# A hybrid decoder layer on one core: the gate product in column groups, work moved to the front, stage offsets redrawn

## The chip, the core and the metric

The kernel runs on one core of one Trainium2 chip. The time is device microseconds of one execution; lower is better. Three executions of the kernel before took 2729.17, 2730.89 and 2732.62 us. A further execution, 2731.02 us long, was taken with the hardware profiler, and all views of the trace come from it.

## What is computed

One decoder layer (DEPTH is 1, so only layer 0 of the reference runs) on x of 2048 tokens by 1024, with a memory of 256 rows. Token mixer (gated DeltaNet, 8 heads of 128) and memory attention (4 heads) share one input projection and one output projection; then come layer norm, an MLP with squared ReLU (1024 to 4096 to 1024), and a second layer norm.

```python
proj = x @ w_in
a = proj[..., 4 * GDN_WIDTH:4 * GDN_WIDTH + GDN_HEADS]
b = proj[..., 4 * GDN_WIDTH + GDN_HEADS:4 * GDN_WIDTH + 2 * GDN_HEADS]
q = l2_normalize(heads(qkv[..., :GDN_WIDTH]))      # qkv after a causal conv and silu
beta = jax.nn.sigmoid(b.astype(jnp.float32))
g = -jnp.exp(a_log) * jax.nn.softplus(a.astype(jnp.float32) + dt_bias)
o = chunk_gated_delta_rule(q, k, v, g, beta)
o = (rms_norm(o, gate_norm_w) * jax.nn.silu(heads(z))).reshape(B, T, GDN_WIDTH)
m = memory_attention(mq, mem_k, mem_v)
return jnp.concatenate([o, m], axis=-1) @ w_out
```

The columns a and b of the projection, 16 in all, are what this text calls the gates: a decay and a write strength for each head and token.

## The kernel before, in words

**Stages.** Tokens are taken in four blocks of 512 (TB); two blocks make a pair. For each block the mixer runs over the 8 heads: `dense` projects q, k and v of a head and convolves them, `gdn_a` and `gdn_b` run the recurrence in chunks of 128, `gate` projects z, and four memory heads stand among them. After two mixers come the output projection (`out_seven`) and the two MLP matrices (`ff1`, `ff2`), each as a seven-product scheme, for the pair. The next pair follows. In the trace the first pair's mixers lie at about 0 to 570 us, its output projection up to about 760, its MLP up to about 1374, and the second pair repeats this.

**Precision.** A float32 operand is split into a high part, rounded to fp32r by ScalarE (`split`, line 555), and a low part, the rest, subtracted by VectorE. A product is three fp32r matmuls, high by high, high by low and low by high (`mm3`, line 573). Products with smaller operands, and all transposes, are plain float32. `T` is the split x of a block, transposed, in eight tiles k of 128 rows each (T_tiles, line 649); a weight pair (high and low) is a tile `whl`, its raw form `wraw` (three buffers). PSUM has banks of 512 columns: three for "acc", one "m", two "pb", and "ga0" and "ga1".

**The gates before.** `gates` (line 726) loads the 16 columns of the weight (w_ab), splits them into a tile abw of 16 high and 16 low columns, and multiplies: for each of the 8 k, abw by high T and by low T, 16 matmuls with 32 weight columns and 512 moving columns, all into partitions 0 to 31 of one acc bank (aab, lines 731 to 734). ScalarE copies the bank to ab, four transposes of 32 by 128 bring it to pab, and two VectorE operations add the parts for high and low weights into gab (lines 742 and 743). A chain of small operations then makes the decays and strengths, and matmuls with a triangle and with ones sum them (pg). All later stages of the block read them.

**The start.** `first_tokens` (line 1587) loads x of block 0 tile by tile, and between the tiles, in three pieces (W0K), q's weights of head 0; it splits each as it comes. `columns` loads four norm vectors and transposes them (pln); then come the gates, and then `mixer`, whose first projection (aq) uses the weights that `first_tokens` brought. k's weights of head 0 come through `load_in` (line 586) when `dense` asks for them: for block 0 this loads the raw weights, splits them and stores the split form (wsc), and other blocks load that.

**Later blocks.** `next_block` (line 1608) has five steps. Steps 0 to 3 load two x tiles each into one wraw buffer and split them; step 4 loads q's weights of head 0 and makes the gates. For blocks 1 and 3 the five steps stand behind the previous mixer; for block 2 they stand inside the last product of the first pair's `ff2`.

**The order of the work.** Nothing is issued as written. A recorder keeps all operations, and `issue` (line 313) plays them through a planner with a cost for each (`cost`, line 272): each engine takes, of the operations whose inputs are ready by the plan, the one with the lowest number. The number is the place in the program plus an offset. `PLACE` (line 190) holds these offsets for named stages, keyed by block, step and letter; `spot` (line 529) switches them. The resulting order is fixed in the program, and each engine runs its list in that order. Almost every operation therefore has line 424 in the trace, and groups are told apart by tile names: aq, ak, av, az and amq are projections, pc, po, pkq, pq and pp belong to the recurrence, ao is the output projection, fA to fC and f2A to f2C the MLP.

Of the kernel before, what the change touches and what calls it, by code (L numbers as in the profile page):

```python
# [184 lines left out]
class Op:  # L185
# [2 lines left out]


PLACE = {  # L190
# [12 lines left out]
}  # L203


class Recorder:
# [64 lines left out]
    @staticmethod  # L271
    def cost(o, name, wr, rd, args, kw):
        e = o.eng
        shapes = [r.shape for r in wr] + [r.shape for r in rd]
        n = max([_prod(s[1:]) for s in shapes] or [1])
        if e == "PE":
            rhs = kw.get("rhs", args[2])
            mo, n = _prod(args[1].shape[1:]), _prod(rhs.shape[1:])
            f32 = name == "transpose" or isinstance(rhs, Ref) and rhs.buf.dtype == F32
            o.load, o.cols, o.lhs = 4 + 0.84 * mo, mo, args[1].buf if isinstance(args[1], Ref) else None  # L280
            o.last = 2.4 + 0.8334 * n if f32 else 13.4 + 0.4167 * n
            if name == "transpose":
                return o.last
            if f32:
                return o.last + max(o.last, o.load)
            return o.last
        psum = any(r.buf.psum for r in rd + wr)
        if e == "SP":
            n = _prod(wr[0].shape if wr else rd[0].shape)
            o.extra = 1700 + n * 4 / 300.0  # L290
            o.late = 2000 if rd and any(s[0] == "partition_broadcast" for s in rd[0].steps) else 300
            return 450
        scal = [v for v in args[2:] if not isinstance(v, (int, float))] if name.startswith("tensor_scalar") else []
        scal += [v for k, v in kw.items() if k in ("scalar", "scalar1", "scale", "bias") and not isinstance(v, (int, float))]
        if e == "ACT":
            n = _prod((wr[0]).shape[1:])
            return 52 + 0.833 * n + (0 if psum else 42) + 93 * len(scal) + ((305 if scal else 198) if "accum_out" in kw else 0)
        if e == "DVE":
            slow = 30 if name in ("transpose", "stream_shuffle") else 0
            fast = not psum and not any(r.perm() for r in rd + wr) and name in ("tensor_copy", "tensor_scalar_mul", "tensor_scalar_add", "tensor_scalar_max",  # L300
                                         "memset")
            return 68 + slow + (0.52 if fast else 1.042) * n + 62 * len(scal) + (7 * n if name == "reciprocal" else 0)
        if name == "memset":
            return 40 + 0.83 * n
        if kw.get("op") == ALU.pow:
            return 460 + 165 * n
        if name == "tensor_copy":
            return 120 + 0.83 * n
        if name == "affine_select":
            return 125 + 0.9 * n  # L310
        return 150 + 2.1 * n if name == "tensor_tensor" else 296 + 3.34 * n
# [129 lines left out]
def hybrid_layer(  # L441
# [46 lines left out]
    def small(name, shape, bufs=3, dt=F32):  # L488
        return rec.buf(sm, shape, dt, name, bufs, name)

    def bank(name, tag):
        return rec.buf(ps, (P, TB), F32, tag, PBUFS[tag], name)
# [39 lines left out]
    state = [rec.buf(cst, (P, P), F32, "state%d" % h, 1, "state") for h in range(H)]  # L532
    for h in range(H):
        nc.gpsimd.memset(state[h], 0.0)
    lnc = rec.buf(cst, (P, 4 * KT), F32, "lnc", 1, "lnc")
    nea = rec.buf(cst, (P, H), F32, "nea", 1, "nea")
    halo = rec.buf(cst, (P, 24, 3), F32, "halo", 1, "halo")
# [185 lines left out]
                                  in_=st[i].bitcast(F32).rearrange("p (h e) -> p h e", h=MH))  # L723


    def gates(b, T):
        raw = small("abraw", [P, KT, 16], 1)
        nc.sync.dma_start(out=raw, in_=w_ab.rearrange("p (k f) -> p k f", k=KT))
        w = small("abw", [P, KT, 32], 1, F32R)
        split(raw, w[:, :, :16], w[:, :, 16:])  # L730
        a = bank("aab", "acc")
        for k in range(KT):
            nc.tensor.matmul(a[:32], w[:, k], T_of(T, 0, k), start=k == 0, stop=False)
            nc.tensor.matmul(a[:32], w[:, k], T_of(T, 1, k), start=False, stop=k == KT - 1)
        ab = slot("ab", "th")
        nc.scalar.copy(out=ab[:32], in_=a[:32])
        pab = bank("pab", "m")
        for c in range(NC):
            nc.tensor.transpose(pab[:, c * 32:(c + 1) * 32], ab[:32, c * P:(c + 1) * P], ident[:32, :32])
        pc = pab[:, :P].rearrange("p (c f) -> p f c", c=NC)  # L740
        pv = small("gab", [P, 16, NC], 1)
        nc.vector.tensor_copy(pv, pc[:, 16:])
        nc.vector.tensor_tensor(out=pv, in0=pc[:, :16], in1=pv, op=ALU.add)
        sh = [P, H, NC]
        if b == 0:
            alog = small("alog", [P, H], 1)
# [76 lines left out]
    def dense(b, h, T, G, w0=None):  # L823
        res = {}
        for nm, o in (("q", QO), ("k", KO), ("v", VO)):
            w = w0 if w0 and nm == "q" else load_in(b, o // P + h)
            a = bank("a" + nm, "acc")
            project(a, w, T)
            c = slot("c" + nm, "d")
# [315 lines left out]
    MEMORY = 1  # L1145
    MEM_AT = {5: 0, 6: 1, 7: 2, 8: 3}

    W0K = {0: 2, 2: 4, 4: 8}

# [435 lines left out]
        nc.vector.tensor_copy(lnc, pt[:, :4 * KT])  # L1585

    def first_tokens():
        T = T_tiles()
        rt = rec.buf(wp, (P, KT, P), F32, "wraw", NR, "wraw")
        wt, hi, lo = pair()  # L1590
        hi, lo = hi.rearrange("p (k f) -> p k f", k=KT), lo.rearrange("p (k f) -> p k f", k=KT)
        for k in range(KT):
            if k % 2 == 0:
                xj = tok_tile("xj").rearrange("p (k f) -> p k f", k=2)
            if k in W0K:
                w = slice(k, W0K[k])
                kw = range(k, W0K[k])
                nc.sync.dma_start(out=rt[:, w].part(*kw), in_=w_in[0].rearrange("p (k f) -> p k f", k=KT)[:, w])
                split(rt[:, w].part(*kw), hi[:, w].part(*kw), lo[:, w].part(*(100 + i for i in kw)))
            xk = xj[:, k % 2].part(k % 2)  # L1600
            nc.sync.dma_start(out=xk, in_=xtd[:, k, 0:TB])
            split(xk, T_of(T, 0, k), T_of(T, 1, k))
        nc.sync.dma_start(out=wsc[0], in_=wt.bitcast(F32))
        return T, ([hi[:, k].part(k) for k in range(KT)], [lo[:, k].part(100 + k) for k in range(KT)])

    ahead = {}

    def next_block(b, step):

        if b >= NB:  # L1610
            return
        if step < 4:
            if step == 0:
                ahead["T"] = T_tiles()
            k = 2 * step
            xj = rec.buf(wp, (P, 1024), F32, "wraw", NR, "xj").rearrange("p (k f) -> p k f", k=2)
            nc.sync.dma_start(out=xj, in_=xtd[:, k:k + 2, b * TB:(b + 1) * TB])
            split(xj, *(t[step] for t in ahead["T"]))
        else:
            ahead["w0"] = load_in(b, 0)  # L1620
            ahead["G"] = gates(b, ahead["T"])


    def mixer(b, T, w0, G):
# [184 lines left out]
    for s in range(NB // 2):  # L1809
# [5 lines left out]
        for i in range(2):  # L1815
            b = 2 * s + i
            if b == 0:
                T, w0 = first_tokens()
                columns()
                G = gates(b, T)  # L1820
            else:
                T, w0, G = ahead["T"], ahead["w0"], ahead["G"]
            mixer(b, T, w0, G)
            if i == 0:
                for k in range(5):
                    next_block(b + 1, k)
# [59 lines left out]
```

## Time and profile before

| what | value |
|---|---|
| three runs, median (lowest to highest) | 2730.89 us (2729.17 to 2732.62) |
| the profiled execution | 2731.02 us |
| its span in the trace | 2729.3 us |
| instructions in the span | 42448 |
| mean granted TensorE clock | 0.999 |
| HBM traffic over the span | 224 GB/s |

The span runs from the first instruction to the last; the remaining 1.7 us lie around it. PE is TensorE's matmuls, PEld its weight loads, which overlap them; DVE is VectorE, ACT is ScalarE, POOL is GpSimd, SP is the queue that issues nearly all DMAs. A busy time is the union of an engine's instructions. A matmul's own duration is its latency; in a row of them the distance between two starts is what each costs.

### The profile page before, as it was taken

The page shows a single profiled execution, that of the slowest core. Times are in us where ns is not written, and L with a number is a line of the kernel's source. Part 1 is how long each engine was busy: PE and PEld are TensorE (multiplying, and loading weights), DVE is VectorE, ACT ScalarE, POOL GpSimd, SP SyncE. Part 2 cuts the span into 40 slices and gives each one's busy share as a digit, 9 for nine tenths or more (in the row PEclk, how much of TensorE's full clock was granted, in tenths as well). Part 3 has the DMA queues.
Part 4 walks back from the last instruction along what each step waited for, and adds up shares of the span by engine and source line. Part 5 has one row for each costly group of instructions (what it writes and reads, how often), then busy time and mean ns, then how long its engine had stood idle before and what let it go on. Part 6 is the DMA issues. An engine that isn't in the chain of part 4 may idle for free.

```text
span 2729.3 us, 42448 instructions
## 1 busy us (share of the span) xinstructions
PE 2707.3 (99%) x13605; PEld 2265.5 (83%) x13605; DVE 2106.6 (77%) x5644; ACT 1634.3 (60%) x4106; POOL 414.5 (15%) x1030
## 2 busy tenths in 40 slices
PE   9999999999999999999999999999999999999998
PEld 7888888888888888888888888888887888888887
DVE  7999889998877777655778887888878666567575
ACT  7778767776475555333446676777756655553341
POOL 3233223321000000000023221332201000000000
PEclk9999999999999999999999999999999999999999
DMA  8666548867787879765754445345678643476673
GB/s 321 232 222 229 206 177 293 309 244 267 264 307 282 296 271 311 261 219 194 263 212 147 140 163 185 140 147 173 217 264 287 228 165 137 162 277 224 212 237 114
DMA packets 208543, 613.99 MB, mean 225 GB/s; under 512 B 23072, under 2 KB 32192, under 8 KB 188352
## 3 DMA queue, kind: packets, MB, share of 16 engines
q1 hardware_dynamic: 207888, 611.23, 63.7%
q8 instruction: 107, 1.75, 0.3%
q14 instruction: 116, 0.95, 0.1%
q10 hardware_dynamic: 432, 0.05, 0.0%
HBM read 436.54 MB, written 174.65 MB: 224 GB/s over the span
## 4 chain that ended last, share of the span: by engine, by line
PE 92%; DVE 3%; ACT 3%; POOL 1%; issue 1%; DMA 1%; DVEq 0%; SPq 0%; POOLq 0%; ACTq 0%
PE f2A L424 13%; PE fA L424 13%; PE ao L424 8%; PE f2C L424 6%; PE fC L424 6%; PE av L424 6%; PE aq L424 6%; PE ak L424 6%; PE az L424 5%; PE f2B L424 3%; PE fB L424 3%; PE amq L424 3%; PE pc L424 3%; PE po L424 2%; PE pkq L424 2%; PE pq L424 1%
## 5 line engine op out<-in xcount | busy, mean ns | idle before, releaser
L424 DVE TENSOR_TENSOR whl<-wraw,whl 128x512 fp32r<-128x512 f32 (+2 forms) x294 | 257.0, 884 | 112.5 <-ACT whl L424 109.6
L424 ACT CAST whl<-wraw 128x512 fp32r<-128x512 f32 (+2 forms) x294 | 226.6, 780 | 158.6 <-PE fC L424 54.6
L424 PE MATMUL fA<-B,whl 128*128 128x512 f32 x1152 | 278.9, 389 | 0.0
L424 ACT CAST X<-X 128x1024 fp32r<-128x1024 f32 x118 | 123.9, 1052 | 231.2 <-DMA X<-xsc 203.2
L424 PE MATMUL f2A<-whl,X 128*128 128x512 f32 x1152 | 262.1, 389 | 0.0
L424 PEld LDWEIGHTS fA<-B,whl 128*128 128x128 f32 x1152 | 216.1, 188 | 45.3 <-DVE B L424 0.3
L424 PEld LDWEIGHTS f2A<-whl,X 128*128 128x128 f32 x1152 | 216.3, 188 | 44.8
L424 DVE TENSOR_TENSOR X<-X,X 128x1024 fp32r<-128x1024 f32 x118 | 144.0, 1221 | 128.8 <-ACT X L424 128.8
L424 PE MATMUL aq<-T,whl 128*128 128x512 f32 x768 | 216.5, 409 | 6.5 <-ACT T L424 5.5
L424 PE MATMUL av<-T,whl 128*128 128x512 f32 x768 | 221.9, 405 | 1.0 <-DVE Bc L424 1.0
L424 PE MATMUL az<-T,whl 128*128 128x512 f32 x768 | 222.8, 404 | 0.0
L424 PE MATMUL ak<-T,whl 128*128 128x512 f32 x768 | 210.8, 405 | 0.0
L424 PE MATMUL fC<-B,whl 128*128 128x512 f32 x768 | 186.8, 389 | 0.4 <-DVE B L424 0.4
L424 PE MATMUL f2C<-whl,X 128*128 128x512 f32 x768 | 174.7, 389 | 0.0
L424 PEld LDWEIGHTS fC<-B,whl 128*128 128x128 f32 x768 | 144.0, 188 | 31.0 <-DVE B L424 0.8
L424 PEld LDWEIGHTS f2C<-whl,X 128*128 128x128 f32 x768 | 144.2, 188 | 29.9
L424 PEld LDWEIGHTS aq<-T,whl 128*128 128x128 f32 x768 | 136.8, 191 | 28.7 <-ACT T L424 5.5
L424 PEld LDWEIGHTS av<-T,whl 128*128 128x128 f32 x768 | 137.8, 189 | 24.2 <-ACT mst L424 1.4
L424 PEld LDWEIGHTS ak<-T,whl 128*128 128x128 f32 x768 | 137.3, 189 | 23.5
L424 PEld LDWEIGHTS az<-T,whl 128*128 128x128 f32 x768 | 137.9, 189 | 22.3
L424 POOL TENSOR_SCALAR ve<-mv 128x1 f32<-128x1 f32 x34 | 16.8, 493 | 918.3 <-DVE mv L424 917.8
L424 PE MATMUL ao<-whl,X 128*128 128x512 f32 x528 | 139.9, 404 | 0.3 <-DVE whl L424 0.3
(294 smaller groups left out, 6294.3 us busy)
## 6 DMA issues: line engine op xcount, KB each, us to landing
whl<-wsc SPq DMA_DIRECT2D x108, 1024.0 KB, 4.9
wraw<-in_w_ff_dram SPq DMA_DIRECT2D x106, 512.0 KB, 4.4
X<-xsc SPq DMA_DIRECT2D x96, 512.0 KB, 3.9
wsc<-whl SPq DMA_DIRECT2D x36, 1024.0 KB, 6.5
whl<-tsc SPq DMA_DIRECT2D x64, 512.0 KB, 4.6
xsc<-hB SPq DMA_DIRECT2D x96, 256.0 KB, 3.8
xo<-cat SPq DMA_DIRECT2D x80, 256.0 KB, 4.3
wraw<-in_w_in_dram SPq DMA_DIRECT2D x35, 512.0 KB, 6.0
```

The costliest lines, as they stand in the source:

```text
L424: o.fn(*[res(a) for a in o.args], **{k: res(v) for k, v in o.kw.items()})
```

## The change

There are four edits.

1. **The gate product.** `gate_rows` multiplies the raw float32 x tiles, not their split form, by the 16 weight columns, padded with zeros to 32, as plain float32 matmuls. Of the 8 tiles k, tile k goes to partitions 32 (k mod 4) to 32 (k mod 4) + 31 of the bank, so four column groups of TensorE are used in turn, and each accumulates two k. `gates` then copies all 128 rows, transposes four times 128 by 128, and four VectorE reductions add the four groups. The weights are loaded once into a constant tile, which GpSimd clears first; their split is gone. In blocks 1 and 3 the products come in two batches of four, after steps 1 and 3; in block 2, in one batch of eight after step 3, and x comes there in eight single tiles in "s0" slots; in block 0, in one batch after the eighth tile.
2. **Ten constant matmuls** (ones by ones, 128 columns, float32) stand first in `first_tokens`, into the bank "m".
3. **k's weights of head 0** are loaded, split and stored in `first_tokens`, behind x tile 4, and not in `dense`.
4. **The offsets in `PLACE`** are another set. The planner's cost of a float32 matmul with 32 weight columns and 512 moving columns becomes a quarter of the former.

```diff
 PLACE = {
-    ('w',): 445, (0, 0, 'F'): -65, (0, 1, 'Y'): 285, (0, 2, 'D'): -5, (0, 2, 'Y'): -225, (0, 2, 'n'): 600,
...
+    ('w',): 440, (0, 0, 'F'): -215, (0, 0, 'H'): -140, (0, 0, 'n'): -20, (0, 1, 'H'): -145, (0, 14, 'F'): 320,
...
 }
@@
+            if f32 and mo == 32 and n == 512:
+                return (o.last + max(o.last, o.load)) / 4
@@
+    abw = rec.buf(cst, (P, KT, 32), F32, "abw", 1, "abw")
+    nc.gpsimd.memset(abw, 0.0)
@@
-    def gates(b, T):
-        raw = small("abraw", [P, KT, 16], 1)
-        nc.sync.dma_start(out=raw, in_=w_ab.rearrange("p (k f) -> p k f", k=KT))
-        w = small("abw", [P, KT, 32], 1, F32R)
-        split(raw, w[:, :, :16], w[:, :, 16:])
-        a = bank("aab", "acc")
-        for k in range(KT):
-            nc.tensor.matmul(a[:32], w[:, k], T_of(T, 0, k), start=k == 0, stop=False)
-            nc.tensor.matmul(a[:32], w[:, k], T_of(T, 1, k), start=False, stop=k == KT - 1)
+    def gate_rows(a, xs, ks):
+        for k, x in zip(ks, xs):
+            q = slice(32 * (k % 4), 32 * (k % 4) + 32)
+            nc.tensor.matmul(a[q], abw[:, k], x, start=k < 4, stop=k >= 4)
+
+    def gates(b, a):
         ab = slot("ab", "th")
-        nc.scalar.copy(out=ab[:32], in_=a[:32])
+        nc.scalar.copy(out=ab, in_=a)
         pab = bank("pab", "m")
         for c in range(NC):
-            nc.tensor.transpose(pab[:, c * 32:(c + 1) * 32], ab[:32, c * P:(c + 1) * P], ident[:32, :32])
-        pc = pab[:, :P].rearrange("p (c f) -> p f c", c=NC)
+            nc.tensor.transpose(pab[:, c * P:(c + 1) * P], ab[:, c * P:(c + 1) * P], ident)
         pv = small("gab", [P, 16, NC], 1)
-        nc.vector.tensor_copy(pv, pc[:, 16:])
-        nc.vector.tensor_tensor(out=pv, in0=pc[:, :16], in1=pv, op=ALU.add)
+        for c in range(NC):
+            nc.vector.tensor_reduce(out=pv[:, :, c], in_=pab[:, c * P:(c + 1) * P].rearrange("p (j f) -> p f j", j=4)[:, :16],
+                                    op=ALU.add, axis=AX.X)
@@
-            w = w0 if w0 and nm == "q" else load_in(b, o // P + h)
+            w = w0[nm] if w0 and nm in w0 else load_in(b, o // P + h)
@@
-    W0K = {0: 2, 2: 4, 4: 8}
+    W0K, W1K, WARM = {0: 2, 2: 4, 4: 8}, 4, 10
@@
     def first_tokens():
-        T = T_tiles()
+        a = bank("warm", "m")
+        for _ in range(WARM):
+            nc.tensor.matmul(a[:, :P], ones, ones, start=True, stop=True)
+        T, xs = T_tiles(), []
...
             split(xk, T_of(T, 0, k), T_of(T, 1, k))
+            xs.append(xk)
+            if k == W1K:
+                wk = load_in(0, KO // P)
+        nc.sync.dma_start(out=abw[:, :, :16], in_=w_ab.rearrange("p (k f) -> p k f", k=KT))
+        ahead["ab"] = bank("aab", "acc")
+        gate_rows(ahead["ab"], xs, range(KT))
@@
             if step == 0:
-                ahead["T"] = T_tiles()
+                ahead["T"], ahead["x"], ahead["ab"] = T_tiles(), [], bank("aab", "acc")
             k = 2 * step
-            xj = rec.buf(wp, (P, 1024), F32, "wraw", NR, "xj").rearrange("p (k f) -> p k f", k=2)
-            nc.sync.dma_start(out=xj, in_=xtd[:, k:k + 2, b * TB:(b + 1) * TB])
-            split(xj, *(t[step] for t in ahead["T"]))
+            c = slice(b * TB, (b + 1) * TB)
+            if b % 2:
+                xj = rec.buf(wp, (P, 1024), F32, "wraw", NR, "xj").rearrange("p (k f) -> p k f", k=2)
+                nc.sync.dma_start(out=xj, in_=xtd[:, k:k + 2, c])
+                split(xj, *(t[step] for t in ahead["T"]))
+                ahead["x"] += [xj[:, j] for j in range(2)]
+                batch = 4
+            else:
+                for j in range(2):
+                    xj = slot("xj", "s0")
+                    nc.sync.dma_start(out=xj, in_=xtd[:, k + j, c])
+                    split(xj, *(T_of(ahead["T"], i, k + j).part(j) for i in range(2)))
+                    ahead["x"].append(xj)
+                batch = KT
+            n = len(ahead["x"])
+            if n % batch == 0:
+                gate_rows(ahead["ab"], ahead["x"][n - batch:], range(n - batch, n))
         else:
-            ahead["w0"] = load_in(b, 0)
-            ahead["G"] = gates(b, ahead["T"])
+            ahead["w0"] = {"q": load_in(b, 0)}
+            ahead["G"] = gates(b, ahead["ab"])
```

More of the change, by code (lines that the diff above doesn't have):

```diff
@@ L1602, in first_tokens @@
             split(xk, T_of(T, 0, k), T_of(T, 1, k))
+            xs.append(xk)
[4 more added lines that the diff above has]
+        gate_rows(ahead["ab"], xs, range(KT))
         nc.sync.dma_start(out=wsc[0], in_=wt.bitcast(F32))
-        return T, ([hi[:, k].part(k) for k in range(KT)], [lo[:, k].part(100 + k) for k in range(KT)])
+        return T, {"q": ([hi[:, k].part(k) for k in range(KT)], [lo[:, k].part(100 + k) for k in range(KT)]), "k": wk}
     ahead = {}
@@ L1819, in hybrid_layer @@
                 columns()
-                G = gates(b, T)
+                G = gates(b, ahead["ab"])
             else:
```

22 rows, old and new, of the table PLACE are left out of this document.

## The prediction

> **What bounds the kernel now.** I read the page first, then one table of busy time by stage, then TensorE's waits, then the chain of work that ended last.
>
> ```profile
> span 2729.3 us, 42448 instructions
> PE 2707.3 (99%) x13605; PEld 2265.5 (83%) x13605; DVE 2106.6 (77%) x5644; ACT 1634.3 (60%) x4106; POOL 414.5 (15%) x1030
> PE 92%; DVE 3%; ACT 3%; POOL 1%; issue 1%; DMA 1%; DVEq 0%; SPq 0%; POOLq 0%; ACTq 0%
> ```
>
> TensorE is busy for 2707.3 of 2729.3 us, so what it is given to do and how densely it does it is the time. The table by stage (columns: length, then busy us and instructions of PE, PEld, DVE, ACT, POOL, the granted clock, DMA share, GB/s) says where the other 22.0 us lie:
>
> ```profile
> 0.00:15.00 15.00, 9.45 (x31) 6.47 (x32) 9.52 (x23) 8.88 (x16) 5.42 (x26) 1.00 0.76 261
> 15.00:760.00 745.00, 739.83 (x4106) 624.64 (x4105) 664.75 (x2284) 535.38 (x1643) 203.07 (x490) 1.00 0.71 252
> 760.00:1374.00 614.00, 613.61 (x2727) 506.27 (x2726) 428.72 (x620) 308.13 (x452) 10.53 (x21) 1.00 0.76 263
> 1374.00:2120.00 746.00, 744.31 (x4098) 631.84 (x4097) 616.16 (x2195) 497.42 (x1588) 184.82 (x477) 1.00 0.54 192
> 2700.00:2729.30 29.30, 20.06 (x89) 16.29 (x87) 18.05 (x30) 0.00 (x0) 6.29 (x8) 0.90 0.19 72
> ```
>
> About 5.6 us go before the first matmul, 9.2 us in the last normalisation and store, and between them 5.2 us in the mixers of the first pair of blocks and 1.7 us in those of the second. The waits of TensorE, longest first (total us, times, longest), confirm that none is large but the first:
>
> ```profile
> PE aq L424 <- ACT T L424: 5.5, 1, 5.5
> PE ao L424 <- ACT whl L424: 1.1, 1, 1.1
> ```
>
> So a microsecond of TensorE's work removed is worth close to a microsecond of span, and work that goes off other engines is worth nearly nothing. The profiled execution took 2731.02 us around its span of 2729.3, and the median of the three runs is 2730.89; the sum is made against 2731.0.
>
> **The gate product: removed.** Two pieces of the chain give TensorE's pace, and the rows of the tiles aab, pab and gab what the gates issue:
>
> ```profile
> 1119.70 43.52 PE f2C L424 x192
> 1359.06 3.65 PE aab L424 x16
> L424 PE MATMUL aab<-T,abw x64: 387/396/479, 13.6 to 1673.7; 128*32 128x512 f32 x64
> L424 PE MATMUL pab<-ident,ab x16: 220/222/246, 18.6 to 1689.8; 32*128 32x32 f32 x16
> L424 DVE COPY gab<-pab x4: 217/222/224, 20.4 to 1690.0; 128x64 f32<-128x64 f32 x4
> L424 DVE TENSOR_TENSOR abw<-abraw,abw x4: 279/284/291, 12.9 to 1363.6; 128x128 fp32r<-128x128 f32 x4
> ```
>
> 43.52/192 is 0.227 us for an fp32r matmul of 512 columns; the gates' 16 take 3.65, 0.228 each, although they fill 32 of 128 columns. The duration of one (0.39) is latency; the spacing is the cost. All 64 go: -64 x 0.228 = **-14.6**. The four small transposes of each block go as well. What they cost is not their width:
>
> ```profile
> 1363.23 0.61 PE L424 MATMUL f2A<-whl,xh 128*128 128x512 f32 x2
> 1363.78 0.43 PE L424 MATMUL pab<-ident,ab 32*128 32x32 f32 x4
> 1364.14 0.50 PE L424 MATMUL f2A<-whl,xl 128*128 128x512 f32 x1
> 1364.48 0.62 PE L424 MATMUL f2A<-whl,xh 128*128 128x512 f32 x2
> ```
>
> The second f2A of the first row starts at 1363.46; from there to 1364.48 are 1.02 us, of which two f2A explain 0.45. The excursion costs 0.57, and only about 0.21 of it lies between the starts of the four (0.43 less one latency of 0.22): the other 0.36 is lost going in and coming out. Four times: **-2.3**. Removed in all: -16.9.
>
> **The gate product: added.** Per block there are 8 plain float32 products of 512 columns. What a float32 pass costs:
>
> ```profile
> L424 PE MATMUL pc<-R,Y 128*128 128x128 f32 x256 | 49.8, 276 | 0.4 <-DVE R L424 0.3
> L424 PE MATMUL pt<-ident,y 128*128 128x128 f32 x128 | 20.1, 272 | 0.0
> 2114.37 0.60 PE L424 MATMUL pt<-ident,y 128*128 128x128 f32 x4
> ```
>
> The code makes 128 products R by Y (8 heads, 4 chunks, 4 blocks), and the trace has 256 of them: a float32 product is two passes; a transpose is one. Four transposes take 0.60: (0.60 - 0.272)/3 = 0.109 per pass of 128 columns, so 0.437 for 512, and 64 passes come to 28.0 us one after the other. No row of before shows four column groups side by side. The bounds are 28.0 (no overlap) and 7.0 (all four). I take full overlap within a run of products that nothing interrupts, because the four groups share neither weights nor output partitions, and each reads its own x. How long such runs are, block 1 shows, where the gates were planned between other work:
>
> ```profile
> 321.71 0.40 PE L424 MATMUL aab<-T,abw 128*32 128x512 f32 x1
> 322.73 1.87 PE L424 MATMUL aab<-T,abw 128*32 128x512 f32 x7
> 324.58 0.47 PE L424 MATMUL aab<-T,abw 128*32 128x512 f32 x1
> 327.39 1.32 PE L424 MATMUL aab<-T,abw 128*32 128x512 f32 x5
> 328.69 0.70 PE L424 MATMUL aab<-T,abw 128*32 128x512 f32 x2
> ```
>
> Sixteen came in five runs there, in one run in blocks 0 and 2. After the change odd blocks issue two batches of four; I take one of them as broken, so three runs per odd block, each two passes deep (0.87): 2 x 3 x 0.87 = 5.2. Even blocks: one run of eight, four passes deep: 2 x 1.75 = 3.5. The four transposes per block are now 128 wide: 16 x 0.109 = 1.7. Added: 10.5. Net **-6.4**.
>
> Going into and out of column groups may also cost: between 0, as for aab, which has the same 128 by 32 weights and is spaced 0.228 from its neighbours, and 0.36 a run, as for pab; eight runs would make +2.9. I take 0, aab being the nearer row. The Trainium skill ("TensorEngine Tiling (Array Packing)", Key Properties) speaks against this: a change of tiling mode drains TensorE. By that rule the sum would end 2.9 higher, near 2726; the trace shows such a loss for 32-row tiles and none for 32 columns starting at column 0.
>
> **The start.** Three edits act there, so I read the first 25 us:
>
> ```profile
> 7.30 2.33 PE L424 MATMUL aq<-T,whl 128*128 128x512 f32 x5
> 10.72 1.30 PE L424 MATMUL aq<-T,whl 128*128 128x512 f32 x5
> 9.54 2.15 DVE L424 TENSOR_TENSOR T<-xj,T 128x512 fp32r<-128x512 f32 x3
> 12.34 0.68 DVE L424 TENSOR_TENSOR T<-xj,T 128x512 fp32r<-128x512 f32 x1
> 14.29 1.05 ACT L424 CAST whl<-wraw 128x1024 fp32r<-128x1024 f32 x1 [1.78 <-DMA wraw<-in_w_in_dram]
> 15.38 1.23 DVE L424 TENSOR_TENSOR whl<-wraw,whl 128x1024 fp32r<-128x1024 f32 x1 [2.07 <-ACT whl L424]
> 23.45 5.60 PE L424 MATMUL av<-T,whl 128*128 128x512 f32 x24
> 5.00:10.00 5.00, 4.45 (x10) 3.30 (x11) 4.70 (x11) 4.33 (x8) 1.07 (x4) 1.00 1.05 383
> ```
>
> Five matmuls take 2.33 us at 7.3 and 1.30 at 10.7: the array is slow at first. Ten constant products are 20 passes; at the early pace (2.33/1.30 of 0.109, 0.20 us) they take about 4 us, and the slow stretch falls into the 5.5 us in which TensorE has nothing to do. That alone gains little, since the splits of x set the pace: VectorE is busy 4.70 of 5 us and DMA is full (383 GB/s), and the last T comes at 13.02. From 5.55 to 23.45 TensorE does 24 aq, 24 ak, 16 aab and the pab: 64 x 0.227 + 0.57 = 15.1 in 17.9 us, a loss of **2.8**, the most that can be had. Against it, k's weights are 512 KB put in SP's queue ahead of x 5 to 7 (1.4 us at 383 GB/s), with a split of 1.05 on ScalarE and 1.23 on VectorE ahead of theirs, so these T come up to 1.4 later; but ak then fills TensorE while they are awaited. Between -2.8 and +1.4 I take **-0.6**: the VectorE row is the nearest, its work is moved and not removed. If the cover by ak fails, the +1.4 shows whole.
>
> **Edits costed at nothing.** The splits of abw go (0.28 on VectorE a block) and four reductions of 64 elements replace two operations of 0.22: at most +0.4 a block in the gates' chain, behind TensorE's other products; without that cover it is +1.7 in all. Block 2 takes x in eight pieces, beside the last product of the second feed-forward matrix, where TensorE hardly waits (613.61 of 614 us busy). The memset of abw lies on POOL, and three loads of the gate weights leave SP. A new wait: in odd blocks the raw x tiles (two of three wraw buffers) are free only when TensorE has read them, and one of three acc banks is held from the first batch to ab's copy; SP's queue behind the next raw load, and the ScalarE split behind that, wait with it. TensorE's projections cover this; if not, it is the last rival below.
>
> **Redrawn offsets.** They reorder the mixers everywhere. The gain is bounded by the idle between start and tail, about 7; for a loss no row is a bound. If the first pair idled as little as the second, 3.5 would be gained; as much could be lost. I take **-1**. Sum: 2731.0 - 6.4 - 0.6 - 1.0 = **2723**.
>
> **The rivals.**
> *Two deep.* A product's second pass needs the columns of its first. If TensorE starts matmuls strictly in order, group 1's first pass waits behind group 0's second, and a run of n products takes n+1 passes: even blocks 2 x 9 x 0.437 = 7.9, odd ones (runs of 4, 2, 2) 2 x 11 x 0.437 = 9.6, with transposes 19.2, so +2.3 in place of -6.4: 2731.7. For it: all matmul starts in the rows above are in order. Against it: nothing shows that a waiting pass holds up another group. The Trainium skill ("TensorE: Matmul & The Clock Gate", Part 3) states this order: matmuls start and end in program order. It also has a packing of three column groups at 2.38 times, for one-pass products; no run here shows either for float32.
> *No overlap (slower).* The groups run one after another: 28.0 + 1.7 - 16.9 = +12.8, so 2742. It decides below an overlap of 28.0/(16.9 - 1.7 + 1.6) = 1.67. For it: aab used a quarter of the columns at full price. Against it: aab's 16 all used the same columns.
> *The order stalls.* The product gains, but offsets and held buffers make both pairs idle more: if each lost a further 4.4 us, +8.7 for -1, 2733. It turns the result from 7 us of new idle on. For it: the first pair idles three times as long as the second; against it: TensorE's longest wait in a mixer is 1.1.
>
> **How the numbers follow.** Full overlap 0.62, two deep 0.20, no overlap 0.10, the order stalls 0.08. A measurement of this kernel can tell about 0.2%, 5.5 us, from no change: 2725.4 to 2736.4 counts as the same. Full overlap lies around 2723 with some 4 us either way: 0.50 faster, 0.12 the same. Two deep: 0.02, 0.13, 0.05. No overlap: 0.10 slower. Stalls: 0.05 and 0.03. In sum 0.52, 0.30, 0.18. The low end is every bound at its best, 2731 - 6.4 - 2.8 - 7.3 = 2714; the high end is the two-deep case with start (+1.4) and order (+3.5) at their worst, 2738. The no-overlap case stays outside.
>
> **What would show it.** Float32 aab passes in groups that start together, a batch of four taking about 0.9 us; 2.2 would say two deep, 3.5 no overlap. Gaps of 0.3 before and after a run say that the drain counts. The av matmuls should start before 21.5 us. Idle in 15 to 760 above 5.2 would show the order as the loser. I am wrong most plainly if aab's busy time grows while the start is unchanged.

## The result, and the profile after

The changed kernel takes 2726.21 us (median; 2724.67 to 2728.48) beside 2731.82 of the kernel before in the same series. The ratio is 0.9981, with a 95% interval from 0.9974 to 0.9987: faster by 0.2%, 5.6 us. The forecast was 2723, with 2714 to 2738 as the range; it counted 2725.4 to 2736.4 as no change and gave that 0.30, against 0.52 for a gain, and 2726.21 lies in this band, 0.8 us from its end. The profiled execution has a span of 2724.2 us, 5.1 less than before. The page's head, busy time by engine and the chain by engine:

```profile
span 2724.2 us, 42520 instructions
PE 2708.0 (99%) x13625; PEld 2264.0 (83%) x13625; DVE 2104.8 (77%) x5652; ACT 1632.0 (60%) x4106; POOL 422.5 (16%) x1031
PE 89%; DVE 6%; ACT 2%; DMA 1%; POOL 1%; issue 1%; DVEq 0%; SPq 0%; ACTq 0%; POOLq 0%
```

TensorE is busy 0.7 us longer than before in a span 5.1 us shorter. That is no contradiction: 4.6 us of it are the constants, in time that was idle. Busy time by stage, with the same columns as before:

```profile
0.00:15.00 15.00, 12.60 (x55) 8.38 (x55) 10.27 (x22) 8.74 (x15) 5.69 (x27) 1.00 0.79 254
15.00:760.00 745.00, 741.82 (x4112) 625.25 (x4109) 665.32 (x2288) 536.93 (x1640) 209.27 (x490) 1.00 0.71 253
1374.00:2120.00 746.00, 744.64 (x4106) 631.53 (x4105) 616.78 (x2199) 499.68 (x1598) 181.39 (x475) 1.00 0.55 194
```

The idle of the first pair falls from 5.2 to 3.2 us, that of the second from 1.7 to 1.4. The gate product itself is seen in the chain around block 2, where it stands among products of the MLP, and in TensorE's timeline of block 1 (start, length, what, count):

```profile
1344.78 12.47 PE f2A L426 x55
1357.24 1.85 PE aab L426 x16
1359.10 1.37 PE f2A L426 x5
1360.47 0.44 PE pab L426 x4
```

```profile
315.31 1.91 PE L426 MATMUL aab<-xj,abw 128*32 128x512 f32 x10
317.14 0.49 PE L426 MATMUL po<-state,qd 128*128 128x128 f32 x2
317.56 1.04 PE L426 MATMUL aab<-xj,abw 128*32 128x512 f32 x2
...
327.66 1.05 PE L426 MATMUL aab<-xj,abw 128*32 128x512 f32 x4
```

Sixteen passes of 0.437 us are done in 1.85 us of the chain, where before the sixteen fp32r matmuls took 3.65. But a run of two passes (one product) takes as long as one of four. To charge each run with all that it costs, I took the time from the start of the matmul ahead of it to the second start behind it, and subtracted what these two cost otherwise (0.2275 for 512 columns, 0.119 for 256, 0.109 for 128 in float32). In the raw trace the passes of a run start 0.007 us apart in fours, and the fours follow each other after 0.43.

| | block 0 | block 1 | block 2 | block 3 | transposes | sum |
|---|---|---|---|---|---|---|
| before: aab, us | 3.74 | 3.80 | 3.65 | 3.73 | 2.27 | 17.2 |
| after: aab, us | 2.16 | 4.49 | 2.06 | 3.66 | 2.06 | 14.4 |
| runs after (products) | 8 | 5, 1, 2 | 8 | 4, 2, 2 | | |

A run of up to four products costs 1.18 to 1.28, one of five to eight 2.06 to 2.16. With 0.43 per four passes abreast, that leaves about 0.32 us a run for going in and out. So the gate product gives **2.8 us**: 3.2 in blocks 0 and 2 and 0.3 in block 3 and the transposes, less 0.7 that block 1 lost, where the planner broke the product into three runs. The rest of the 5.1 us lies elsewhere. Two marks help to place it, the first matmul of q of head 1 in block 0 and the last matmul of all; before first, then after:

```profile
28.89 1.29 PE L424 MATMUL aq<-T,whl 128*128 128x512 f32 x5
2719.67 0.39 PE L424 MATMUL f2A<-whl,xl 128*128 128x512 f32 x1
```

```profile
28.04 1.30 PE L426 MATMUL aq<-T,whl 128*128 128x512 f32 x5
2714.70 0.39 PE L426 MATMUL f2A<-whl,xl 128*128 128x512 f32 x1
```

### The profile page after: what moved, and what is told of

Same layout as the page of the kernel before. It is cut to its first block, busy times and chain, and to the rows that moved or that the text cites. A ratio compares the mean times of both kernels' runs of the same rounds, so it can differ in the third digit from the quotient of the medians.

```text
span 2724.2 us, 42520 instructions
## 1 busy us (share of the span) xinstructions
PE 2708.0 (99%) x13625; PEld 2264.0 (83%) x13625; DVE 2104.8 (77%) x5652; ACT 1632.0 (60%) x4106; POOL 422.5 (16%) x1031
## 4 chain that ended last, share of the span: by engine, by line
PE 89%; DVE 6%; ACT 2%; DMA 1%; POOL 1%; issue 1%; DVEq 0%; SPq 0%; ACTq 0%; POOLq 0%
PE f2A L426 13%; PE fA L426 12%; PE ao L426 8%; PE f2C L426 6%; PE fC L426 6%; PE az L426 6%; PE ak L426 6%; PE aq L426 6%; PE av L426 5%; PE fB L426 3%; PE f2B L426 3%; PE pc L426 3%; PE amq L426 3%; PE po L426 2%; PE pkq L426 1%; PE pq L426 1%
## 5 line engine op out<-in xcount | busy, mean ns | idle before, releaser
L426 PE MATMUL av<-T,whl 128*128 128x512 f32 x768 | 211.6, 402 | 0.0
L426 POOL TENSOR_SCALAR ve<-mv 128x1 f32<-128x1 f32 x34 | 15.6, 460 | 906.1 <-DVE mv L426 893.8
```

Of the source, the lines that this page charges most:

```text
L426: o.fn(*[res(a) for a in o.args], **{k: res(v) for k, v in o.kw.items()})
```

## The experiments

Twelve kernels were run, in three series after that of the changed kernel. The kernel before ran in each; its medians were 2731.82, 2731.97, 2731.41 and 2732.16 us, so a difference under 1 us between kernels of different series says little. The last two columns are against the kernel before in the same series.

| kernel | us (median) | us from before | ratio to before, 95% interval |
|---|---|---|---|
| the changed kernel | 2726.21 | -5.6 | 0.9981 (0.9974 to 0.9987) |
| gate product alone, old offsets | 2746.87 | +14.9 | 1.0056 (1.0043 to 1.0069) |
| changed, old offsets | 2744.35 | +12.4 | 1.0052 (1.0038 to 1.0066) |
| changed, old gate product | 2749.04 | +17.1 | 1.0064 (1.0051 to 1.0076) |
| changed, no constants | 2726.32 | -5.7 | 0.9979 (0.9970 to 0.9988) |
| changed, k in dense | 2727.31 | -4.1 | 0.9985 (0.9976 to 0.9994) |
| changed, one column group | 2755.11 | +23.7 | 1.0087 (1.0073 to 1.0101) |
| changed, group k//2 | 2729.07 | -2.3 | 0.9992 (0.9984 to 1.0001) |
| changed, batches gathered | 2722.80 | -8.6 | 0.9969 (0.9957 to 0.9981) |
| before, no offsets | 2736.49 | +4.3 | 1.0014 (1.0005 to 1.0023) |
| changed, no offsets | 2735.43 | +3.3 | 1.0011 (1.0002 to 1.0021) |
| gathered, no constants | 2721.95 | -10.2 | 0.9964 (0.9952 to 0.9977) |
| changed, margin 105 | 2741.85 | +9.7 | 1.0036 (1.0023 to 1.0050) |

**Which part brings the gain?** Theory A said the gate product; theory B the redrawn offsets. Three kernels exchange one part each, by putting the old table, or the old product, in the other kernel:

```diff
-    ('w',): 440, (0, 0, 'F'): -215, (0, 0, 'H'): -140, (0, 0, 'n'): -20, (0, 1, 'H'): -145, (0, 14, 'F'): 320,
+    ('w',): 445, (0, 0, 'F'): -65, (0, 1, 'Y'): 285, (0, 2, 'D'): -5, (0, 2, 'Y'): -225, (0, 2, 'n'): 600,
...
```

The gate product alone (the old table, WARM = 0, no `wk` in `first_tokens`):

> The new gate product in the kernel before: old offsets, no constant matmuls, k's weights in their old place. The trace of the changed kernel has the gate passes in groups of four that start within 0.02 us of each other, and the gaps at the gate product and its transposes sum to 15.6 us against 19.5 before. Theory A (the gate product brings most of the 5.6 us): 3 to 5 us faster than before, with at least 1.5 us in each of blocks 0 and 2. Theory B (the redrawn offsets bring it, the gate product alone loses its gain to broken runs and to losses going in and out): within 1.5 us of before.

The changed kernel with the old table:

> The changed kernel with the offsets of before; gate product, constant matmuls and the early k weights stay. Theory A: 4 to 6 us faster than before, so about the changed kernel's time. Theory B: no faster than before by more than 1.5 us, since the old offsets belong to another order of work.

The changed kernel with `gates` and `next_block` of before:

> The changed kernel with the gate product of before (16 fp32r matmuls of 32 columns per block, into one column group); the start and the new offsets stay. Theory A: 3 to 5 us slower than the changed kernel, so 1 to 2 us faster than before. Theory B: about the changed kernel's time, 4 us or more faster than before.

All three took 2744 to 2749 us, 12 to 17 slower than before. Theory A misses all three; theory B holds only for the second, where it forecast no more than the absence of a gain. Each had priced the parts as if they could be exchanged. (By the account above, the 15.6 and 19.5 us that the first text starts from are 14.4 and 17.2.) In the traces the product nearly keeps its price (15.7 and 15.8 us with its transposes in the first two, 17.0 in the third), so it isn't the product that is slower. The changed kernel with the old table shows where the time went. First its waits of TensorE, then the two stages with the mixers:

```profile
PE amk L426 <- DVE mT L426: 2.4, 1, 2.4
PE ao L426 <- DVE whl L426: 2.1, 2, 1.8
PE ak L426 <- ACT whl L426: 1.5, 2, 1.1
PE ptv L426 <- ACT Y L426: 1.3, 5, 0.4
```

```profile
15.00:760.00 745.00, 737.22 (x4064) 616.98 (x4054) 659.08 (x2277) 528.91 (x1628) 197.98 (x488) 1.00 0.70 248
1374.00:2120.00 746.00, 742.12 (x4077) 628.31 (x4077) 616.64 (x2209) 489.71 (x1571) 184.74 (x475) 1.00 0.52 187
```

Idle of 7.8 and 3.9 us in place of 3.2 and 1.4, in many small waits with different releasers. Take the distance between two matmul starts, less the shortest that any of the traces has for the same two shapes; what is over 0.1 us of it, without the neighbours of the gate product, sums to 14.7 us in these two stages of the changed kernel (15.5 before), and to 26.4 in this one.

Part of this is TensorE's clock. The same stretch of the first mixer, in this kernel and then in the changed one (the granted clock stands third from the end):

```profile
83.20:89.90 6.70, 5.37 (x11) 3.33 (x12) 6.70 (x27) 2.25 (x4) 1.25 (x1) 0.50 0.37 131
```

```profile
83.20:89.90 6.70, 6.70 (x42) 5.98 (x41) 6.24 (x27) 1.84 (x3) 0.19 (x1) 1.00 1.00 382
```

TensorE was busy for 4.75 of the 7.10 us ahead; then the granted clock is 0.50 from 83.1 to 90.0 us, where matmuls of 512 columns start 0.43 apart, and 0.23 after it. From 12 us to the last matmul, such stretches stand in the traces of all seven kernels that came out slower than before, and in none of the other seven: 6.8 us in the two with the old table, three of 3.4 in the one with the old product, one of 3.4 in the rest. Gaps of over 3 us in all lie in the 6.8 us ahead of each, but the kernel with k in dense has as much around 520 us without a drop, so the gaps alone don't decide it. At half the pace a stretch costs at most half its length, 1.7 to 5.1 us; most of the 18 us by which this kernel is behind the changed one lies elsewhere.

**What is a table of offsets worth?** The empty table takes it out of both kernels:

```diff
-PLACE = {
...
-}
+PLACE = {}
```

> The kernel before with an empty table of offsets. The kernels with a table taken from the other structure took 2744 to 2749 us. Theory E (a table is worth something only for the order that it was drawn with, and a foreign table is about as good as none): 2740 to 2755. Theory F (a table is good by itself and the foreign ones did harm): near 2732.

> The changed kernel with an empty table of offsets. Theory E: 2737 to 2752, so 10 us or more slower than with its own table, and against the kernel before without offsets faster by what the gate product removes from TensorE, 2.8 us in the traces, with a few us either way for the order. Theory F: near 2726.

Neither theory holds as put. Both kernels lose by having no table, but only 4.3 and 8.9 us, and a foreign table is some 9 to 13 us worse than none. Without tables the two structures are 1.1 us apart (2736.49 and 2735.43), with intervals that overlap, although the gate product costs 14.6 against about 17.5 us in their traces. The rest of those 2.9 us is lost again elsewhere: q of head 1 starts at 28.63 before and 28.64 after, and the last matmul at 2724.02 and 2724.22. How finely a table is bound to one order, the last kernel of this question shows; it moves a constant by which the planner lengthens waits:

```diff
-MARGIN, TURN = 100, 40
+MARGIN, TURN = 105, 40
```

> The changed kernel with one constant of the planner moved: the margin that it adds to a wait between engines, 105 ns for 100. No operation changes, only the order that is planned. Theory E, in its strong form, says that a table fits one order exactly, so 2735 or more; if the table fits the structure and small shifts of order do little, as when k's weights went back to dense (2727.3), within 3 us of 2726.

It took 2741.85 us, some 15 more than the changed kernel, with no operation different. Its mixers idle for 8.1 and 3.8 us:

```profile
15.00:760.00 745.00, 736.90 (x4086) 618.18 (x4078) 661.69 (x2280) 532.38 (x1632) 204.78 (x488) 1.00 0.70 250
1374.00:2120.00 746.00, 742.24 (x4086) 627.95 (x4085) 614.56 (x2202) 489.67 (x1577) 185.16 (x477) 1.00 0.53 188
```

Another 1.7 us are lost ahead of the first av (24.30 us, against 22.60): the granted clock is 0.50 from 12.7 to 16.1 us, and block 0's gate product costs 3.4 us in place of 2.2. So the strong form holds here, but not always, as the kernel with k in dense shows below. The orders of this program that were run spread over some 20 us, and each table stands for one of the good ones.

**The start.** The constants were left out without touching the order, by planning them and issuing nothing:

```diff
             nc.tensor.matmul(a[:, :P], ones, ones, start=True, stop=True)
+            rec.ops[-1].fn = lambda *args, **kw: None
```

> The changed kernel without its ten constant matmuls, which are still planned but not issued, so that the order of everything else is the same. The first projections would run at the slow spacing of 0.43 us up to about 9.5 us again. If x's splits set the pace there, as the prediction has it, the change in time is under 0.5 us; if the slow clock sets it, TensorE falls behind by up to 2 us, and the av products start at 24.5 instead of 22.6 us.

Same time (2726.32). First TensorE's start in the changed kernel, then without the constants:

```profile
1.19 4.63 PE L426 MATMUL warm<-ones 128*128 128x128 f32 x20 [1.19 <-POOL mhalf L513]
5.48 0.79 PE L426 MATMUL aq<-T,whl 128*128 128x512 f32 x1
6.46 3.54 PE L426 MATMUL aq<-T,whl 128*128 128x512 f32 x12 [0.20 <-DVE T L426]
10.23 0.73 PE L426 MATMUL aq<-T,whl 128*128 128x512 f32 x2 [0.23 <-DVE T L426]
11.51 0.73 PE L426 MATMUL ak<-T,whl 128*128 128x512 f32 x2 [0.55 <-ACT whl L426]
```

```profile
6.46 4.91 PE L426 MATMUL aq<-T,whl 128*128 128x512 f32 x14 [0.18 <-DVE T L426]
11.58 0.73 PE L426 MATMUL ak<-T,whl 128*128 128x512 f32 x2 [0.21 <-ACT whl L426]
```

With the constants the aq matmuls are 0.23 us apart from 7.4 us on, so TensorE is ahead and then waits for the splits (0.20, 0.23 and 0.55 us); without them the spacing is 0.43 until 9.6 us, and it waits less. By 11.6 us both stand at the same place, as the prediction had it: the splits set the pace, of x and here of k's weights (`ACT whl`). The first av starts at 22.60 and 23.00; 0.30 of this difference is a wait for the copy ab at 17.7 us, after the clocks have come level. The other edit of the start, undone:

```diff
-            if k == W1K:
-                wk = load_in(0, KO // P)
```

> The changed kernel with k's weights of head 0 loaded in dense again; constants, gate product and new offsets stay, and the planner orders the rest anew. Two things are read. The start: if the early k weights delay x's last tiles and their splits, as the kernel with the gate product alone suggests (its first av at 21.75 us, against 23.53 with the early start and the same offsets), the first av comes 0.5 to 2 us earlier than the 22.60 of the changed kernel; if the early k fills TensorE usefully, it comes later. The total: theory C (offsets fit one order of work only, and any edit that moves the order loses 10 us or more) says 2736 or more; theory D (the old offsets were merely worse than the new) says within 2 us of 2726.

2727.31 us, 1.1 more (1.5 by the column against before, with intervals that overlap), and theory C falls for this order: it is new and good. The first av came 0.4 earlier (22.18), in the direction expected of a delay by the early weights and just short of the 0.5 forecast, but two matmuls later TensorE waited 1.6 us for av's own weights (this view ends at 25 us):

```profile
22.18 0.61 PE L426 MATMUL av<-T,whl 128*128 128x512 f32 x2
24.43 0.97 PE L426 MATMUL av<-T,whl 128*128 128x512 f32 x3 [1.63 <-DVE whl L426]
```

so that q of head 1 started at 29.57 in place of 28.04. Under the old table that mark came later with the early k and the constants (28.97, against 28.32 in the kernel with the gate product alone). What moving k brings by itself stays open, within some 1.5 us either way.

**Do the column groups overlap, and how deep?** All products in one group:

```diff
-            q = slice(32 * (k % 4), 32 * (k % 4) + 32)
-            nc.tensor.matmul(a[q], abw[:, k], x, start=k < 4, stop=k >= 4)
+            nc.tensor.matmul(a[:32], abw[:, k], x, start=k == 0, stop=k == KT - 1)
```

The copy, the transposes and the sum are cut to the 32 rows.

> The changed kernel with all eight products of a block in one column group (partitions 0 to 31), so that no two passes can overlap; the planner's price stays a quarter. 64 passes of 0.437 us one after the other are 28 us in place of the 12.4 of the changed kernel's trace: 15 to 17 us slower than the changed kernel, with starts 0.43 us apart. If a pass with 32 columns were short by itself and the groups brought nothing, the gate product would cost what it costs now. What the new order adds on top is open.

28.9 us slower than the changed kernel. The product costs 30.3 us by the account above (12.4 with four groups): 17.9 of the 28.9. The other 11 are put down to the order, planned with a price that is no longer true; no run separates them. Going in and out costs here what it does in four groups: a run of one product takes 1.18 us in both. Next, neighbours in the same group, at exactly the same order of work on all engines:

```diff
-            q = slice(32 * (k % 4), 32 * (k % 4) + 32)
-            nc.tensor.matmul(a[q], abw[:, k], x, start=k < 4, stop=k >= 4)
+            q = slice(32 * (k // 2), 32 * (k // 2) + 32)
+            nc.tensor.matmul(a[q], abw[:, k], x, start=k % 2 == 0, stop=k % 2 == 1)
```

> The changed kernel with tile k in column group k//2 and not k mod 4: two products in a row use the same group; every engine's order of work is the same. If a pass that waits for its columns holds up only its own group, blocks 0 and 2 cost what they did (2.1 us each), block 3's runs of 4, 2, 2 products become 2.1 each (6.2 for 3.7) and block 1's 5.3 for 4.5: 3 to 4 us slower than the changed kernel. If it holds up everything behind it, the passes are all but serial: 28 us plus 0.3 per run in place of 12.4, 15 to 18 us slower.

2.9 us slower (3.3 against before in its own series), as the first reading says: runs of 4, 2, 2 products in block 3 cost 2.05, 2.04 and 2.13, and the run of eight in block 2 cost 2.08, against 2.06 in the changed kernel. The chains around block 2, first with one group, then with k//2:

```profile
1361.99 3.85 PE f2A L426 x17
1365.84 6.98 PE aab L426 x16
1372.83 1.36 PE f2A L426 x5
```

```profile
1349.95 8.84 PE f2A L426 x39
1358.79 1.87 PE aab L426 x16
1360.66 1.37 PE f2A L426 x5
```

6.98 is 16 x 0.436: serial. 1.87 is four deep and four abreast, although in program order four passes for group 0 stand ahead of the first for group 1. In the raw trace the first four starts lie 0.013 apart. The trace doesn't name a pass's group, but one group alone is serial, so the four belong to four groups; and block 1's run of five products (groups 0, 0, 1, 1, 2) starts in rows of 3, 3, 2 and 2 passes. A pass that waits for its columns lets the passes behind it go ahead in other columns.

**Is a broken run worth mending?** The planned order is kept, and only a batch's four products are put at the place of the last of them:

```diff
         out.sort(key=lambda o: (o.start, o.i))
+        at = {}
+        for o in out:
+            if o.run is not None:
+                at[o.run] = max(at.get(o.run, 0), o.start)
+        for o in out:
+            o.start = at.get(o.run, o.start)
+        out.sort(key=lambda o: (o.start, o.i))
@@
             nc.tensor.matmul(a[q], abw[:, k], x, start=k < 4, stop=k >= 4)
+            rec.ops[-1].run = id(a.buf), k // 4
```

> The changed kernel with its planned order kept, but the four products of a batch in blocks 1 and 3 put together at the place of the last one. A run of up to four products costs 1.19 us in the trace of the changed kernel, one of eight 2.07. Block 1's runs (2.12, 1.18, 1.19) become two of 1.19, block 3's three (1.20, 1.18, 1.28) two: 3.3 us less than the changed kernel, about 2723. If the products waiting to be gathered only filled time in which TensorE had nothing else, the gain is under 1 us and new idle appears where they stood.

2722.80 us, 3.4 less than the changed kernel's 2726.21 (3.0 by the column against before); the last matmul starts 3.2 us earlier in the trace, and the product's account falls from 12.4 to 9.2. Block 1 has two runs where it had three:

```profile
315.72 1.07 PE L432 MATMUL aab<-xj,abw 128*32 128x512 f32 x8
...
326.11 1.06 PE L432 MATMUL aab<-xj,abw 128*32 128x512 f32 x8
```

No new idle appears where the others stood: TensorE is busy for all 20 us from 310 to 330 in both. In 15 to 760 it idles for 3.8 us, against 3.2; 0.3 of the difference lies before 40 us. The two findings together:

> The changed kernel with gathered batches and without the ten constant matmuls, which are planned but not issued. Gathering took it to 2722.8 and leaving the constants out changed nothing (2726.3 against 2726.2), so 2722 to 2724 if the two edits add; a loss of 1 us or more against 2722.8 would say that the constants do matter at the start.

2721.95 us, a ratio of 0.9964 (0.9952 to 0.9977): the lowest median of the study. Every execution of both gathered kernels lies below every one of the changed kernel. Whether the last 0.9 us (1.6 by the column against before) are real, the overlapping intervals of these two don't say.

## Why the prediction was right, step by step

- **TensorE's work is the time: right, for a fixed order.** What the traces took off the gate product, or added, arrived at the last matmul to within 1 us where the order stayed the same: 3.2 of 3.15 us when the batches were gathered, 3.1 of 4.0 when neighbours shared a group (3.5 in the product, 0.5 in a wait ahead of block 0's transposes). Where the order changed, it need not arrive, as the two kernels without tables show.
- **Removed, -16.9: right.** The account of before gives 17.2.
- **A float32 product is two passes of 0.437, and four groups overlap fully: right.** Fours follow each other after 0.43; one group alone is serial. The rival without overlap falls by the serial starts of the kernel with one group, the two-deep one by the fours of the changed kernel and, more sharply, by the k//2 kernel. The Trainium skill ("TensorE: Matmul & The Clock Gate", Part 3) states that matmuls start and end in program order; across column groups, for float32 products, the starts of the k//2 kernel's trace, 0.013 us apart, speak against it.
- **Going in and out costs 0: this step failed.** It is 0.32 us a run, 2.6 for eight runs, near the upper bound of 0.36 taken from pab. The nearest row, aab, misled: the same shape, but fp32r. That it lay at column 0 is not what made it free, for the kernel with one group has all its float32 products at column 0 and pays the same (1.18 us for a run of one product, 0.87 of it passes). Why the fp32r products pay nothing stays open. The Trainium skill ("TensorEngine Tiling (Array Packing)", Key Properties) has a drain at each change of tiling mode. It was the better guide: a loss of 0.32 us a run agrees with it, though the 32-column fp32r products, with none, show that a reader can't tell from the shape alone where it applies.
- **Three runs per odd block: right in number, short in size.** Block 1's were 5, 1 and 2 products, one step of four more than assumed (0.9), and the transposes cost 2.06 in place of 1.7. With these three terms the sum of -6.4 becomes -2.6; measured -2.8.
- **The start, -0.6: not borne out.** The first head was done 0.85 earlier, but block 0's gate product alone gave 1.5 there, so the rest of the start cost about 0.65, inside the bounds (-2.8 to +1.4). The av matmuls, which were to start before 21.5, started at 22.60. No run shows whose the 0.65 are: without the constants that mark came 0.4 later, and without the early k, in another order, 1.5 later. That the splits set the pace was right.
- **The offsets, -1: too small.** Gate product and start explain 2.1 of the 5.0 us between the last matmuls. What is left, 2.9, is tighter spacing between matmuls that both kernels have, so it came with the new order; how much of it is the offsets, and how much the moved loads and the buffers held longer, no run separates. And the bounds of this term were far too narrow: as much could be lost as the 3.5 that could be gained, the prediction said, and one step of the planner's margin costs some 15. The argument against an order that stalls named 1.1 us as the longest wait in a mixer; that row is ao, the output projection, and the longest in a mixer is 1.0.

The total was near by luck: the gate product was overrated by 3.6 us and the start by some 1.2, and the order underrated by 1.9.

## What to carry to other kernels

When an order of work is planned with offsets drawn for it, an edit cannot be judged by applying it alone: a change of a price or a place can draw a new order, and that draw (here 1 to 15 us) can outweigh the edit (here 3). Hold the order fixed, by changing only what is issued at a planned place, and the edit's own price can be measured, as the constants, the k//2 groups and the gathered batches were. And narrow products pay only in whole runs: a run costs its entry, its exit and full passes even when one group of four is used. Two products in a run took 1.18 to 1.28 us here, in place of four fp32r matmuls of 0.23; four took 1.20, in place of eight.

## What the runs showed of the hardware that was not expected

- Column groups take float32 passes independently: with four passes for one group queued ahead, the other three groups still started 0.013 us apart, and sixteen passes took 1.87 us.
- A run of float32 products of 32 columns costs about 0.32 us to enter and leave, at column 0 alone as in four groups; the 32-row transposes cost 0.36. Sixteen fp32r matmuls of the same shape, at column 0, cost nothing of the kind.
- After gaps that summed to over 3 us in 6.8, the granted clock of a kernel that TensorE bounds fell to 0.50 for 3.4 or 6.8 us in seven traces, and 512-column matmuls went from 0.23 to 0.43 us apart; one trace has such gaps without the drop.
- Wider transposes were no dearer than narrow ones: four of 128 by 128 cost 0.45 to 0.64 us with what lies around them, four of 32 by 128 cost 0.57.
